# Inverse square roots of spread variances by two ACT functions in place of ACT's square root and DVE's reciprocal, in a three-layer hybrid stack on one core

## The chip, the cores and the metric

One core of a Trainium2 chip runs the whole program in one launch. The metric is the device time of that launch in microseconds (us); lower is better. Engines are named as in the profile: PE (TensorE's matmuls), DVE (VectorE), ACT (ScalarE), POOL (GpSimd), SP (SyncE, which issues the DMAs).

## The reference, cut to what matters

512 tokens of width 1024 pass through two hybrid layers (banded attention, a convolution module and retention side by side, an output projection, then an MLP) and a third layer (differential attention and a state-space branch side by side, then a gated feed-forward). Three places divide by a spread, and the change touches those:

```python
def layer_norm(x):                      # convolution module and retention
    mu = jnp.mean(xf, axis=-1, keepdims=True)
    var = jnp.mean(jnp.square(xf - mu), axis=-1, keepdims=True)
    return (xf - mu) * lax.rsqrt(var + EPS)
...
    y = layer_norm(y) * ln_g + ln_b     # convolution: 256 channels, once a layer
...
    y = layer_norm(y).reshape(b, s, RET_WIDTH)   # retention: 64 channels of each of 6 heads
...
    o = rmsnorm(o, subln_gain[i]) * (1.0 - lam_init)   # differential attention: 128 channels of each of 8 heads
```

## The kernel before, in words

Activations of these branches lie with channels on the partitions and the 512 tokens along the free axis. A mean over channels is therefore a matmul with a matrix of ones: `col_sum` (line 1129) splits the squares into a high part `xhi` and a rest `xlo`, and two matmuls (`xhi,ones` and `xlo,ones`, for retention `xhi,blk64` and `xlo,blk64`) leave the variance in PSUM, already spread over all the partitions that need it. What follows is "variance to inverse root", 128x512 each time, at three places:

- `conv_tail` (lines 1236 and 1237, tile `crs`), once in each of the two hybrid layers;
- `ret_pair` (lines 1322 and 1323, tile `rysq`), for three pairs of heads in each hybrid layer;
- `diff_head` (lines 1848 and 1849, a tile `t`), for the eight heads of the third layer.

That makes 2 + 6 + 8 = 16. In each, ACT takes the square root from PSUM with the constant tile `epsc` as bias, and DVE's `reciprocal` turns it over in place; then DVE multiplies (`ry` by `rysq`, `cacc` by `crs`, `osb` by `t`).

All large matmuls are done as three products of high and low parts: weights arrive by DMA as `wraw`, ACT or DVE makes `whi` (a CAST), DVE or POOL the rest `wlo`; activations are `hhi` and `hlo`. These are the main line of the program. The branches named above run beside it as side tasks. Their own tiles are: `stk` and `khi`, `klo` (a head's queries and keys, copied from PSUM), `row` (scores, then their exponentials), `pthi`, `ptlo` (transposed probabilities), `olow` and `o` (output of a head), `cacc`, `csq` (convolution), `ysq`/`rysq` and `ry` (retention), `do`, `osb` (differential attention).

Nothing is issued in program order. `Trace` records every instruction with the time by which it is wanted, `order` (line 443) plays a list schedule through with its own costs, and `issue` (line 642) issues in the order found. So every instruction has line 642 in the profile, and tiles tell them apart. An engine runs its list strictly in that order: one that waits holds up all behind it. Copies and subtractions of split tiles may go to either of two engines, whichever the planner thinks is done first. PE has 4 PSUM slots for the main line and 4 for side tasks.

ACT's functions come in sets, and a load of a set (ACT_TABLE_LOAD) stands ahead of an activation whose function is not in the set loaded. The program's builder places these loads after the order is fixed; the planner estimates them by a table of its own (lines 670 to 679, used at line 577): where the name of the set changes, it adds 1290 ns.

```python
TABLE = {AF.Exp: "exp", AF.Sigmoid: "sigmoid", AF.Silu: "silu", AF.Sqrt: "sqrt", AF.Sin: "sin",
         AF.Gelu_apprx_tanh: "gelu"}
TABLE_LOAD = 1290.0
...
                        f = table(op) if op.eng[1] == "activation" else None
                        if f and f != loaded:
                            c += TABLE_LOAD
                            loaded = f
```

It costs a DVE reciprocal of n columns at 6.26 n + 65 ns, and an activation at 0.833 n plus some tens of ns.

Of the kernel before, what the change touches and what calls it, by code (L numbers as in the profile page):

```python
# [13 lines left out]
AF = mybir.ActivationFunctionType  # L14
# [3 lines left out]
P = 128  # L18
# [206 lines left out]
class View:  # L225
    """A view of a tile that is traced before the tile is placed."""
# [47 lines left out]
    def mask(self):  # L274
        """First and last column, and which ones between unless it's all."""
        c = self.cols.ravel()
        lo, hi = int(c.min()), int(c.max()) + 1
        if hi - lo == c.size:
            return lo, hi, None
        m = np.zeros(self.t.ncols, bool)  # L280
        m[c] = True
        return lo, hi, None if m[lo:hi].all() else m
# [47 lines left out]
class DramView(View):  # L330
    """A view of a tile in DRAM: taken as a whole."""
# [20 lines left out]
class Pool:  # L352
    """Equal slots, which the order of instructions deals out to tiles. Each is a pool of one buffer."""
# [46 lines left out]
class Trace:  # L400
    """Records instructions with the time by which each is wanted, orders them, and issues them."""
# [207 lines left out]
    def room(self, op, new, live, front, state):  # L609
        """Whether slots are free, none is kept for a more urgent instruction, and enough are left  # L610
        for the instructions before in program order."""
# [58 lines left out]
TABLE = {AF.Exp: "exp", AF.Sigmoid: "sigmoid", AF.Silu: "silu", AF.Sqrt: "sqrt", AF.Sin: "sin",  # L670
# [138 lines left out]
class Builder:  # L809
# [132 lines left out]
    # ---------------------------------------------------------------- norms  # L942
# [116 lines left out]
    # ---------------------------------------------------------------- attention helpers  # L1059
# [41 lines left out]
    def v_pack(self, src):  # L1101
        """V of six heads, each as 64 columns of high parts and 64 of low parts."""
        nc = self.nc
        out = []
# [9 lines left out]
    def pv_pair(self, h, pts, V, y):  # L1114
        """One head's output, from the products with the high and the low parts of V below each other."""
        nc = self.nc
# [7 lines left out]
        a = slice(64 * (h % 2), 64 * (h % 2) + 64)  # L1124
        low = self.s2(name="olow")
# [8 lines left out]

    def rows(self, third):
        """Room for the four rows of blocks of a lower triangle."""
        a, b = self.s2(name="row"), self.s2(name="row")
        return [a[:, 384:512], third, a[:, 0:384], b]

    def p_split(self, parts):  # L1140
        """High and low parts by blocks of keys: 512, 384 and twice 256 columns, the last with a block of zeros."""
        out = []
# [8 lines left out]
        last = out.pop()  # L1151
# [48 lines left out]
    # ---------------------------------------------------------------- conv module  # L1200
# [15 lines left out]
    def conv_tail(self, l):  # L1216
        nc = self.nc
# [18 lines left out]
        nc.scalar.activation(rs, var, AF.Sqrt, bias=self.epsc)  # L1236
        nc.vector.reciprocal(rs, rs)
# [11 lines left out]
    # ---------------------------------------------------------------- retention  # L1249
# [29 lines left out]
    def ret_pair(self, p, q, k):  # L1279
# [42 lines left out]
        nc.scalar.activation(ysq, var, AF.Sqrt, bias=self.epsc)  # L1322
        nc.vector.reciprocal(ysq, ysq)
# [13 lines left out]
    # ---------------------------------------------------------------- hybrid layer  # L1337
    def hybrid(self, l):
# [69 lines left out]
        # output projection and residual  # L1408
# [34 lines left out]
    # ---------------------------------------------------------------- MLP  # L1443
# [80 lines left out]
    # ---------------------------------------------------------------- SSM parameters  # L1524
# [158 lines left out]
    # ---------------------------------------------------------------- SSM  # L1683
# [84 lines left out]
    # ---------------------------------------------------------------- differential attention  # L1768
# [21 lines left out]
    def diff_head(self, h, dqk, V):  # L1790
# [57 lines left out]
        nc.scalar.activation(sq, var, AF.Sqrt, scale=1.0 / P, bias=self.epsc)  # L1848
        nc.vector.reciprocal(sq, sq)
# [230 lines left out]
```

## Time and profile before

| | us |
|---|---|
| runs of the kernel before | 2184.87, 2181.4, 2181.93 |
| their median | 2181.93 |
| span of the profiled execution, first to last instruction | 2185.0 |
| PE busy in it | 2065.8 |
| DVE busy | 1395.2 |
| ACT busy | 928.5 |
| POOL busy | 745.5 |

The profiled execution's own time outside its span isn't given; its span of 2185.0 us stands beside the slowest of the three runs (2184.87 us) and 3.1 us over the median. Busy times are sums over one execution. An engine's share of the whole says little here, because the program goes through stages with different limits: the stages with the 16 places of the change are 130 to 190 us (hybrid layer 0), 780 to 840 us (hybrid layer 1) and 1460 to 1710 us (differential heads).

### The profile page before, as it was taken

Reading aid. Unit: us, or ns where it says so; the run is one execution under the profiler, and the core shown is the slowest. Engines: PE = TensorE matmul, PEld = TensorE weight load, DVE = VectorE, ACT = ScalarE, POOL = GpSimd, SP = SyncE. Lnnn points to the kernel's source line nnn. Section 1 sums busy time; section 2 is a strip of 40 time slices with the busy share of each in tenths; the row PEclk is TensorE's granted clock in tenths of the full one; section 3 lists DMA queues with packets and bytes.
Section 4 is the critical chain, followed back from the end, with each engine's and each line's share of the span. In section 5 each row is a group of like instructions: output and inputs, shape, how many; then the busy total and the mean of one; then the engine's idle time right before and its main releaser. Section 6 shows DMA issues by size and latency. Waiting matters only on the chain. (4 is left out here: it accounts for less than half of the span.)

```text
span 2185.0 us, 27033 instructions
## 1 busy us (share of the span) xinstructions
PE 2065.8 (95%) x9964; PEld 1711.6 (78%) x9964; DVE 1395.2 (64%) x2131; ACT 928.5 (42%) x1521; POOL 745.5 (34%) x858
## 2 busy tenths in 40 slices
PE   7789989899999799989999998999999999999999
PEld 7777878778888777788888877677777788888887
DVE  6999596344457999573444464379888646655545
ACT  3267544232234267454222344456578324433332
POOL 3663357980004663210000115764643431000000
PEclk9999999999999999999999999999999999999999
DMA  5223233332333224133332346222224533333222
GB/s 176 80 78 123 87 116 109 128 127 87 97 114 97 87 68 135 49 107 97 96 97 77 115 133 201 79 80 68 92 82 135 169 96 97 97 96 97 87 87 77
DMA packets 85556, 225.16 MB, mean 103 GB/s; under 512 B 10416, under 2 KB 20400, under 8 KB 85424
## 3 DMA queue, kind: packets, MB, share of 16 engines
q1 hardware_dynamic: 85424, 223.43, 32.4%
q8 instruction: 79, 1.29, 0.3%
q14 instruction: 53, 0.43, 0.1%
HBM read 204.25 MB, written 19.14 MB: 102 GB/s over the span
## 5 line engine op out<-in xcount | busy, mean ns | idle before, releaser
L642 POOL TENSOR_TENSOR wlo<-wraw,whi 128x1024 fp32r<-128x1024 f32 (+1 forms) x156 | 374.5, 2408 | 1068.3 <-ACT whi L642 824.9
L642 ACT CAST whi<-wraw 128x1024 fp32r<-128x1024 f32 (+1 forms) x323 | 330.4, 1029 | 726.7 <-PE ps L642 592.1
L642 PE MATMUL ps<-hhi,whi 128*128 128x512 f32 (+1 forms) x1488 | 506.8, 370 | 7.3 <-DVE acc L642 3.1
L642 PE MATMUL ps<-hlo,whi 128*128 128x512 f32 (+1 forms) x1488 | 504.8, 370 | 5.6 <-DVE hlo L642 5.6
L642 PE MATMUL ps<-hhi,wlo 128*128 128x512 f32 (+1 forms) x1488 | 504.3, 369 | 0.3 <-DVE wlo L642 0.3
L642 PEld LDWEIGHTS ps<-hhi,whi 128*128 128x128 f32 x1488 | 272.4, 191 | 54.8 <-issue 4.0
L642 PEld LDWEIGHTS ps<-hlo,whi 128*128 128x128 f32 x1488 | 272.4, 191 | 53.5 <-DVE hlo L642 6.8
L642 PEld LDWEIGHTS ps<-hhi,wlo 128*128 128x128 f32 x1488 | 272.1, 191 | 48.2 <-DVE wlo L642 1.0
L642 DVE TENSOR_TENSOR wlo<-wraw,whi 128x1024 fp32r<-128x1024 f32 x178 | 223.4, 1257 | 114.8 <-ACT whi L642 114.5
L642 PE MATMUL ps<-whi,fhi 128*128 128x512 f32 x688 | 249.7, 392 | 6.1 <-DVE t L642 3.7
L642 PE MATMUL ps<-whi,flo 128*128 128x512 f32 x688 | 249.5, 391 | 0.0
L642 PE MATMUL ps<-wlo,fhi 128*128 128x512 f32 x688 | 249.5, 391 | 0.0
L642 PE MATMUL ps<-wlo,hhi 128*128 128x384 f32 (+1 forms) x448 | 162.7, 380 | 18.3 <-POOL wlo L642 18.1
L642 DVE TENSOR_TENSOR acc<-ps,acc 128x512 f32<-128x512 f32 x112 | 76.5, 687 | 154.7 <-PE ps L642 154.7
L642 PE MATMUL ps<-whi,hhi 128*128 128x384 f32 (+1 forms) x448 | 161.7, 383 | 14.2 <-DVE rotb L642 12.7
L642 PE MATMUL ps<-whi,hlo 128*128 128x384 f32 (+1 forms) x448 | 158.8, 377 | 0.0
L642 PEld LDWEIGHTS ps<-whi,fhi 128*128 128x128 f32 x688 | 129.6, 189 | 34.7 <-DVE t L642 4.2
L642 PEld LDWEIGHTS ps<-wlo,fhi 128*128 128x128 f32 x688 | 129.6, 189 | 27.8
L642 PEld LDWEIGHTS ps<-whi,flo 128*128 128x128 f32 x688 | 129.5, 188 | 27.8
L642 DVE SCALAR_TENSOR_TENSOR cacc<-cy,pv,cacc 128x509 f32<-128x509 f32 (+26 forms) x120 | 125.3, 1088 | 0.6
L642 POOL TENSOR_TENSOR st<-st,mhalf 128x1 f32<-128x1 f32 (+1 forms) x56 | 54.9, 981 | 194.4 <-DVE st L642 190.8
L642 PEld LDWEIGHTS ps<-wlo,hhi 128*128 128x128 f32 x448 | 86.9, 195 | 30.6 <-POOL wlo L642 21.6
(250 smaller groups left out, 3167.8 us busy)
## 6 DMA issues: line engine op xcount, KB each, us to landing
wraw<-in_wst SPq DMA_DIRECT2D x302, 512.0 KB, 3.5
wraw<-in_wst SPq DMA_DIRECT2D x32, 384.0 KB, 3.1
gain<-in_gains SPq DMA_DIRECT2D x20, 256.0 KB, 4.2
X<-in_x SPq DMA_DIRECT2D x16, 256.0 KB, 6.1
xd<-X SPq DMA_DIRECT2D x16, 256.0 KB, 2.0
X<-xd SPq DMA_DIRECT2D x16, 256.0 KB, 4.9
gated<-t SPq DMA_DIRECT2D x16, 256.0 KB, 2.4
gate<-gated SPq DMA_DIRECT2D x16, 256.0 KB, 3.7
```

Of the source, the lines that this page charges most:

```text
L642: getattr(getattr(self.nc, e), m)(*[r(x) for x in op.args], **{k: r(v) for k, v in op.kw.items()})
```

## The change

A helper takes the natural logarithm of variance plus epsilon from PSUM, and then, in place, the exponential of minus half of it, both on ACT. The planner's table names the logarithm's set "exp", as it does the exponential's, and no longer lists the square root. The rest of the difference is removed doc strings.

```diff
-TABLE = {AF.Exp: "exp", AF.Sigmoid: "sigmoid", AF.Silu: "silu", AF.Sqrt: "sqrt", AF.Sin: "sin",
+TABLE = {AF.Exp: "exp", AF.Sigmoid: "sigmoid", AF.Silu: "silu", AF.Ln: "exp", AF.Sin: "sin",
          AF.Gelu_apprx_tanh: "gelu"}
...
+    def rsqrt(self, out, var, scale=1.0):
+        self.nc.scalar.activation(out, var, AF.Ln, scale=scale, bias=self.epsc)
+        self.nc.scalar.activation(out, out, AF.Exp, scale=-0.5)
...
-        nc.scalar.activation(rs, var, AF.Sqrt, bias=self.epsc)
-        nc.vector.reciprocal(rs, rs)
+        self.rsqrt(rs, var)
...
-        nc.scalar.activation(ysq, var, AF.Sqrt, bias=self.epsc)
-        nc.vector.reciprocal(ysq, ysq)
+        self.rsqrt(ysq, var)
...
-        nc.scalar.activation(sq, var, AF.Sqrt, scale=1.0 / P, bias=self.epsc)
-        nc.vector.reciprocal(sq, sq)
+        self.rsqrt(sq, var, 1.0 / P)
```

Since costs and sets are other for the planner, the order of all engines changes from the first of the 16 places on. In the built program the loads of function sets are 41 before and 68 in the change. The planner's choices move 10 of the 323 `whi` casts and 5 of the 8 `hhi<-osb` casts from ACT to DVE, and 4 of 178 `wlo` subtractions from DVE to POOL.

ACT in hybrid layer 0, from the last retention pair's work to the convolution's two SiLUs (`cacc`). The forms with `epsc` are the square roots before, and the logarithms in the change. Before:

```order
L642 ACTIVATE rysq<-ps,epsc 128x512
L642 COPY olow<-o 64x512 x2
L642 ACTIVATE stk<-ps 64x512 x2
L642 CAST whi<-wraw 128x1024
L642 ACTIVATE rysq<-ry 128x512
L642 CAST khi<-ps 64x512
L642 CAST xhi<-rysq 128x512
L642 CAST khi<-ps 64x512 x3
L642 CAST whi<-wraw 128x1024
L642 ACTIVATE rysq<-ps,epsc 128x512
L642 ACT_TABLE_LOAD
L642 ACTIVATE cacc<-cacc,pv 128x512 x2
```

Here the square roots of a pair stand apart, attention's `stk` and `khi` copies between them, with one load, for the SiLU. The change, from the same `xhi<-rysq` to the same SiLUs:

```order
L642 CAST xhi<-rysq 128x512
L642 ACT_TABLE_LOAD
L642 ACTIVATE crs<-ps,epsc 128x512
L642 ACT_TABLE_LOAD
L642 ACTIVATE crs<-crs 128x512
L642 ACT_TABLE_LOAD
L642 ACTIVATE rysq<-ps,epsc 128x512
L642 CAST whi<-wraw 128x1024
L642 ACT_TABLE_LOAD
L642 ACTIVATE rysq<-rysq 128x512
L642 ACT_TABLE_LOAD
L642 ACTIVATE cacc<-cacc,pv 128x512 x2
```

Five loads stand there now, one ahead of every logarithm, every exponential and the SiLUs; the `stk` and `khi` copies of the next attention head have moved behind them. Hybrid layer 1 has the same twelve rows in the same order.

DVE at the same place, from the convolution's inverse root to the first `klo` of the attention head. Before:

```order
L642 RECIPROCAL crs<-crs 128x512
L642 TENSOR_TENSOR ry<-o,olow 64x512 x2
L642 RECIPROCAL rysq<-rysq 128x512
L642 TENSOR_TENSOR xlo<-rysq,xhi 128x512
L642 TENSOR_TENSOR ry<-ry,rysq 128x512
L642 TENSOR_TENSOR cacc<-cacc,crs 128x512 x2
L642 RECIPROCAL rysq<-rysq 128x512
L642 TENSOR_TENSOR mixlo<-cacc,mixhi 128x512
L642 TENSOR_TENSOR ry<-ry,rysq 128x512
L642 TENSOR_TENSOR mixlo<-cacc,mixhi 128x512
L642 SCALAR_TENSOR_TENSOR stk<-ps,stk 64x512 x2
L642 TENSOR_TENSOR klo<-ps,khi 64x512 x4
```

The change:

```order
L642 TENSOR_TENSOR ry<-o,olow 64x512 x2
L642 TENSOR_TENSOR xlo<-csq,xhi 128x512
L642 TENSOR_TENSOR xlo<-rysq,xhi 128x512
L642 TENSOR_TENSOR cacc<-cacc,crs 128x512 x2
L642 TENSOR_TENSOR ry<-ry,rysq 128x512
L642 CAST whi<-wraw 128x1024
L642 TENSOR_TENSOR mixlo<-cacc,mixhi 128x512 x2
L642 SCALAR_TENSOR_TENSOR stk<-ps,stk 64x512 x2
L642 TENSOR_TENSOR klo<-ps,khi 64x512 x4
```

The reciprocals are gone from the list, and DVE takes over a `whi` cast that ACT had.

ACT in the third layer, behind the exponentials of the second differential head. Before:

```order
L642 ACTIVATE row,st<-row,st,rq 128x512
L642 ACT_TABLE_LOAD
L642 ACTIVATE t<-ps,epsc 128x512
L642 ACT_TABLE_LOAD
L642 ACTIVATE t<-ps 128x512
L642 CAST pthi<-ps 128x512
L642 CAST pthi<-ps 128x384 x2
L642 CAST stk<-ps 64x512 x2
L642 CAST whi<-wraw 128x1024
```

The change (`t<-ps,epsc` is the first head's logarithm, `t<-t` its exponential, `t<-ps` the sigmoid of a gate):

```order
L642 ACTIVATE row,st<-row,st,rq 128x512
L642 ACT_TABLE_LOAD
L642 ACTIVATE t<-ps,epsc 128x512
L642 CAST whi<-wraw 128x1024
L642 ACT_TABLE_LOAD
L642 ACTIVATE t<-t 128x512
L642 ACT_TABLE_LOAD
L642 ACTIVATE t<-ps 128x512
L642 CAST stk<-ps 64x512
L642 CAST pthi<-ps 128x512
L642 CAST pthi<-ps 128x384 x2
```

Two loads have become three, with the exponential between them.

## Rows read from the trace of the kernel before

**Rows 1.** The profile page's head: the span, busy time of each engine (share of the span, count of instructions), and the span in 40 slices of 54.6 us, each digit the busy share of a slice in tenths (9 is 90% or more).

```profile
span 2185.0 us, 27033 instructions
PE 2065.8 (95%) x9964; PEld 1711.6 (78%) x9964; DVE 1395.2 (64%) x2131; ACT 928.5 (42%) x1521; POOL 745.5 (34%) x858
PE   7789989899999799989999998999999999999999
DVE  6999596344457999573444464379888646655545
ACT  3267544232234267454222344456578324433332
```

**Rows 2.** Busy time by stretch: from:to, length, then busy us (count of instructions) of PE, PEld, DVE, ACT, POOL, then the granted clock, DMA share and GB/s.

```profile
130.00:190.00 60.00, 57.79 (x282) 47.91 (x281) 57.04 (x83) 46.83 (x81) 36.79 (x66) 0.97 0.27 84
190.00:250.00 60.00, 56.30 (x293) 45.76 (x292) 48.59 (x116) 41.03 (x89) 14.59 (x6) 1.00 0.28 93
780.00:840.00 60.00, 58.63 (x296) 48.39 (x295) 56.68 (x77) 50.31 (x85) 34.99 (x67) 1.00 0.33 103
840.00:900.00 60.00, 52.63 (x263) 42.16 (x261) 52.95 (x120) 42.01 (x91) 19.00 (x8) 0.98 0.26 82
1460.00:1710.00 250.00, 235.89 (x1128) 189.77 (x1128) 212.34 (x398) 171.08 (x320) 118.77 (x84) 1.00 0.31 98
150.00:160.00 10.00, 7.90 (x32) 6.19 (x31) 9.90 (x8) 6.72 (x12) 6.14 (x9) 0.83 0.37 124
210.00:220.00 10.00, 7.26 (x38) 5.23 (x37) 9.78 (x23) 8.20 (x20) 2.40 (x1) 1.00 0.22 73
550.00:600.00 50.00, 50.00 (x220) 40.84 (x219) 21.74 (x25) 13.18 (x16) 2.70 (x1) 1.00 0.31 94
```

**Rows 3.** What PE waited for in 1460 to 1710 us: us in total, times, longest.

```profile
PE ps L642 <- DVE row L642: 7.4, 6, 2.1
PE ps L642 <- DVE klo L642: 2.2, 3, 1.0
...
PE ps L642 <- DVE t L642: 1.4, 1, 1.4
```

**Rows 4.** The same for 840 to 900 us.

```profile
PE ps L642 <- DVE row L642: 3.2, 4, 1.8
PE ps L642 <- DVE klo L642: 2.9, 2, 1.5
```

**Rows 5.** DVE in order of time in hybrid layer 0: start us, us (of all in a merged row), engine, line, op, out<-in, count, idle before and releaser.

```profile
155.03 3.34 DVE L642 RECIPROCAL rysq<-rysq 128x512 f32<-128x512 f32 x1
158.29 1.81 DVE L642 TENSOR_TENSOR ptlo<-ps,pthi 128x512 fp32r<-128x512 f32 x3
161.13 1.79 DVE L642 TENSOR_TENSOR ptlo<-ps,pthi 128x512 fp32r<-128x512 f32 x3 [1.02 <-ACT pthi L642]
```

**Rows 6.** DVE's groups by tile over the whole span: form, count | busy us, mean ns of one | idle before, releaser.

```profile
L642 DVE RECIPROCAL t<-t 128x512 f32<-128x512 f32 x8 | 26.8, 3350 | 3.5 <-ACT t L642 3.5
L642 DVE RECIPROCAL rysq<-rysq 128x512 f32<-128x512 f32 x6 | 20.1, 3350 | 2.4 <-ACT rysq L642 2.3
L642 DVE RECIPROCAL crs<-crs 128x512 f32<-128x512 f32 x2 | 6.7, 3336 | 0.0
L642 DVE CAST whi<-wraw 128x1024 fp32r<-128x1024 f32 x11 | 7.7, 704 | 5.8 <-POOL wlo L642 2.5 <-PE ps L642 1.9 <-issue 1.3
```

**Rows 7.** ACT's groups by tile and form over the whole span, same columns.

```profile
L642 ACT CAST whi<-wraw 128x1024 fp32r<-128x1024 f32 x291 | 304.0, 1051 | 647.1 <-PE ps L642 535.5 <-DVE X L642 61.1 <-issue 37.6
L642 ACT ACT_TABLE_LOAD x41 | 52.6, 1283 | 8.7 <-DVE st L642 7.2 <-PEq L2072 0.8
L642 ACT ACTIVATE t<-t 128x512 f32<-128x512 f32 x64 | 40.5, 633 | 2.0
...
L642 ACT ACTIVATE row<-row,st,rq 128x512 f32<-128x512 f32 x16 | 12.9, 808 | 0.0
...
L642 ACT ACTIVATE t<-ps,epsc 128x512 f32<-128x512 f32 x8 | 5.5, 689 | 1.6 <-PE ps L642 1.5
...
L642 ACT CAST hhi<-osb 128x512 fp32r<-128x512 f32 x8 | 4.7, 627 | 1.4 <-DVE osb L642 0.8 <-PE ps L642 0.6
...
L642 ACT ACTIVATE rysq<-ps,epsc 128x512 f32<-128x512 f32 x6 | 4.1, 688 | 7.5 <-PE ps L642 7.4
```

**Rows 8.** ACT in order of time in hybrid layer 0, columns as in Rows 5.

```profile
148.22 1.99 ACT L642 CAST whi<-wraw 128x1024 fp32r<-128x1024 f32 x2
150.23 1.28 ACT L642 ACT_TABLE_LOAD   x1
151.52 0.69 ACT L642 ACTIVATE rysq<-ps,epsc 128x512 f32<-128x512 f32 x1
...
167.74 1.19 ACT L642 COPY olow<-o 64x512 f32<-64x512 f32 x2 [1.97 <-PE o L642]
...
177.67 1.52 ACT L642 ACTIVATE cacc<-cacc,pv 128x512 f32<-128x512 f32 x2
179.10 1.13 ACT L642 CAST mixhi<-cacc 128x512 fp32r<-128x512 f32 x2
...
181.08 1.19 ACT L642 ACTIVATE stk<-ps 64x512 fp32r<-64x512 f32 x2
...
183.42 1.78 ACT L642 CAST khi<-ps 64x512 fp32r<-64x512 f32 x3
```

## The prediction on record

> **What bounds the kernel now.** I read the page's head first [rows 1]: PE is busy 95% of the span, so a change on ACT and DVE can win only where PE stands still, and lose only by making it stand still more. A slice is 54.6 us: PE reads 7 or 8 in slices 1 to 3, 6, 8, 14, 18 and 25 and 9 elsewhere, too coarse for our places, but DVE reads 8 or 9 just there (slices 2 to 4, 14 to 16 and 28 to 31: 55 to 218, 710 to 874, 1475 to 1693 us) and in slice 6, while ACT reads 8 once and 7 or less elsewhere.
>
> So next I cut the span at the stages of the 16 inverse roots [rows 2]. Length less PE's busy time is PE's idle time: 2.2 us in 130 to 190, 1.4 us in 780 to 840, 14.1 us in 1460 to 1710, together 17.7 us. Behind the first two, where attention's side tasks run out, PE idles another 3.7 us (190 to 250) and 7.4 us (840 to 900). These 28.8 us are all that the change can win directly. DVE is the fullest of the helpers there: 95% and 94% of the first and third of these stretches, 85% of the heads' 250 us, against 78%, 84% and 68% for ACT.
>
> Who ends PE's waits says the same. In the heads' stretch it is DVE's `row`, `klo` and `t`, 11.0 of the 14.1 us [rows 3]; behind hybrid layer 1 `row` and `klo`, 6.1 of 7.4 [rows 4]. No wait of weight there is put down to ACT. A DVE reciprocal is long (3.34 us) and the list is strict: in layer 0 three `ptlo` subtractions start at 158.29, when the reciprocal in front of them ends, and the next three stand behind those [rows 5].
>
> **What DVE loses.** 16 reciprocals, 26.8 + 20.1 + 6.7 = 53.6 us [rows 6]: 13.4 us in each hybrid layer, 26.8 us in the heads. The planner gives DVE ten more `whi` casts at 704 ns, 7.0 us [rows 6], and five `hhi` casts.
>
> **What ACT gains.** A logarithm in place of a square root: the trace has no logarithm. Its nearest row is the square root itself, same shape, PSUM source and `epsc` bias, 688 to 689 ns [rows 7]; so nothing is added, and I bound the difference by 0.1 us either way. The exponential in place: nearest is the 128x512 square from SBUF, 633 ns; the long end is the `row` exponential with two pointers, 808 ns [rows 7]. I take 0.63: 16 x 0.63 = 10.1 us. Loads: 68 - 41 = 27 more at 1.283 us = 34.6 us [rows 7]. Together 44.7 us; the casts that move away take 10 x 1.05 + 5 x 0.63 = 13.6 us off again [rows 7]. Net ACT +31, DVE -44 (and a few `wlo` that go to POOL): the two come nearer to each other, and the question is what PE sees.
>
> **How dear a load is.** In rows, a load follows the cast in front of it within 0.02 us and the activation starts 1.29 us after the load did [rows 8]; no other gap is there. The Trainium skill (ScalarE: Activation LUTs, section What ACT_TABLE_LOAD costs) has the same 1283 ns, but adds a drain of about 1380 ns to each switch; by that page, an estimate, 27 loads would cost ACT 72 us, which speaks against the change, and the rows do not bear it out. The sum goes by the rows' 1.29.
>
> **What the planner does not see.** Its table now puts logarithm and exponential in one set. The built order has a load ahead of nearly every one of either. Going through the 68 loads by the planner's table leaves 43, so 25 are not in its plan: 7 in each hybrid layer and 11 in the heads. PE's list is laid out for a plan in which ACT is earlier.
>
> **Hybrid layers, by hand.** From the end of the third pair's `xhi` the new ACT list runs: 5 loads 6.45, 2 logarithms 1.38, 2 exponentials 1.26, one `whi` 1.05, two SiLUs 1.52, two `mixhi` 1.13, two `stk` 1.19, two of the four `khi` 1.19 [rows 7, 8]; 15.2 us, less about 0.6 for the overlap that two casts show (1.99 us for two of 1.05). So attention's first scores can start after some 14.6 us. PE's new list has 42 matmuls from that `xhi` to these scores; at the full stages' 220 in 50 us [rows 2] PE is there in 9.5 us. It waits about 5.1 us. Before that, the logarithm and exponential of the second pair, a load and two `olow` stand ahead of the convolution's `xhi`: 0.69 + 1.29 + 0.63 + 1.19 + 0.64, with handovers some 4.6 us, against 20 smaller matmuls, 3.9 us: a wait of 0.7. Each layer: 5.8 us of idle in place of 2.2 and 1.4, so **+3.6 and +4.4 us**.
>
> What comes back: in PE's list the last value product of attention now stands 3.7 us (layer 0) and 8.6 us (layer 1) of matmuls earlier than before, since the plan has a freer DVE. The idle stretches behind, 3.7 and 7.4 us [rows 2], are mostly waits for DVE at the tail of these tasks. I take back half: **-1.9 and -3.7 us**; bounds are none and all of it.
>
> **Heads.** 11 unplanned loads are 14.2 us. ACT is only 68% full here, its gaps absorb some, and sigmoids of gates have slack, so I let half reach PE: **+7.1**. Of PE's 14.1 us of idle, waits for DVE behind chains that reciprocals shared; I take half: **-7.1**. Bounds are 0 to 14 for each.
>
> The moved casts have their cover: `whi` is made ahead in four buffers, and 0.70 us on DVE takes the place of 1.05 on ACT; should that cover go, ten times 0.7 us is at stake. Work outside these stretches keeps its durations.
>
> **Sum.** 3.6 + 4.4 - 1.9 - 3.7 + 7.1 - 7.1 = +2.4 us. PE's idle also moves its clock: in 150 to 160 us it idled 2.1 us and the mean grant was 0.83, between the 1.2 and 2.4 GHz levels, in 210 to 220 it idled 2.7 us and the grant was 1.00 [rows 2]. At 0.83 ten microseconds lose 1.7 us of work. Waits of 5 us in one piece are longer than today's there, so I add one such loss: **+4.1 us**. From the profiled span, 2185.0, that gives 2189.1; that execution stands 3.1 us over the median of the runs, so on the median 2181.9 + 4.1 = **2186.0 us**. 0.2% is 4.4 us, about what a measurement of this kernel tells from no change.
>
> **Rivals.**
> *All loads reach PE (0.24).* ACT becomes the bound in the hybrid clusters and each unplanned load in front of `khi` or the exponentials is a wait. Mechanism and price: 3.6 + 4.4 + 3.4 for the clock, nothing back at the tails, 14.2 in the heads: +25.6, 2207 at worst; with half of the DVE relief in the heads, +18.5, 2200. For it: ACT's 14.6 us against PE's 9.5. Against: ACT at 171 of 250 us in the heads. It decides where the loads of a head stand ahead of its exponentials with no gap behind them. This is the other side of the next one.
>
> *DVE's relief wins (0.20).* Waits for DVE go: two thirds of 14.1 + 3.7 + 7.4 is -16.8, and the clusters cost only 2 us a layer because DVE, no longer in 3.35 us pieces [rows 6], catches up: -13, 2169. For it: DVE's 94 to 95% and the releasers [rows 3, 4]. Against: PE idles only 2.2 and 1.4 us in the very stretches of the hybrid layers' reciprocals.
>
> *The loads cost nothing (0.03).* Were the 25 unplanned loads not to run, or to be no-ops because the set is there already, each cluster would shrink by 5 x 1.29 = 6.5 us, so its wait and the clock's 1.7 us vanish, and with them the heads' +7.1: -3.6 - 3.7 - 1.9 - 7.1 + 0.7 = about -16, 2166. Against: the built order has the loads, and every one of the 41 in the trace takes its 1283 ns [rows 7]. The Trainium skill (ScalarE: Activation LUTs, section Table sets: the hidden batching unit) says that one set holds both functions, so that the pair needs one load; this rule would give that time, and the built order contradicts it.
>
> *A load holds ACT twice as long (0.03).* If something behind each load took as long again, 1.28 us, five in each cluster would add 6.4 us to PE's wait in each layer and half of 17 more loads in the heads 10.9: 4.1 + 12.8 + 10.9 = +27.8, 2210. Against: the activation that starts 1.29 us after its load [rows 8]. The skill's drain, from above, is this case.
>
> **Numbers.** My forecast (0.50) is a trade with a small loss: within 0.2% for 0.36, slower by more for 0.13, faster by more for 0.01. Slower: 0.13 + 0.24 + 0.03 = 0.40. Faster: 0.01 + 0.18 (the relief; its weak end, 0.02, stays within) + 0.03 = 0.22. Within: 0.36 + 0.02 = 0.38. The range goes from most of the relief case to the milder slower case: 2172 to 2200. The forecast's own range is 2179 to 2193.
>
> **What would show it.** ACT_TABLE_LOAD x68 at 1283 ns with no gap behind; no 128x512 RECIPROCAL; ACT near 960 us, DVE near 1350. In 130 to 200 and 780 to 850 us PE should wait some 5 us at attention's first scores, released by ACT's `khi` or DVE's `klo` behind it. The tails behind should idle less than 3.7 and 7.4 us. In the heads, PE's waits for `row` and `klo` should be about as long as before. I am wrong if PE's idle in the hybrid stretches stays under 2.5 us a layer (ACT's lag is absorbed), if that of the heads falls below 7 us or grows past 20, or if the time moves by idle of PE in stages that have none of the 16.

## The result: slower by 1.15%, and the profile after

The changed kernel takes **2208.99 us** (median, 2207.67 to 2210.25) where the kernel before takes 2183.4 beside it (2181.4 to 2189.26): ratio 1.0115, 95% interval 1.0099 to 1.013. The forecast was 2186.0 us in a range of 2172 to 2200. It was wrong. All medians here are of fast executions; two slow ones, of 2539 us (old heads, below) and 10196 us (the kernel before), are left out.

The head of the page after, with the slices that answer to [rows 1]:

```profile
span 2208.3 us, 27033 instructions
PE 2078.8 (94%) x9964; PEld 1727.7 (78%) x9964; DVE 1368.8 (62%) x2124; ACT 961.1 (44%) x1551; POOL 755.4 (34%) x862
PE   7788989999999788999999998989999999999999
DVE  6987586444447987463444564468778646655555
ACT  3277534222234277544322344447579424433322
```

The span is 23.3 us longer. TensorE's 9964 matmuls are the same, yet its busy time rises by 13.0 us (2078.8 - 2065.8) and its idle time by only 10.3 us (129.5 - 119.2). More than half of the loss is the same matmuls taking longer, not waiting; the mean granted clock over the span is 0.974 where it was 0.983.

The stretches that answer to [rows 2] (length, busy us and count of PE, PEld, DVE, ACT, POOL, then the granted clock, DMA share, GB/s), and the loads of ACT's tables, which answer to [rows 7]:

```profile
130.00:190.00 60.00, 53.53 (x253) 44.02 (x252) 41.14 (x77) 50.63 (x79) 31.60 (x58) 0.94 0.21 62
190.00:250.00 60.00, 54.17 (x274) 44.71 (x273) 51.57 (x112) 41.30 (x95) 14.22 (x7) 0.94 0.30 100
780.00:840.00 60.00, 54.91 (x273) 46.36 (x271) 42.28 (x69) 51.34 (x82) 36.95 (x76) 0.94 0.20 62
840.00:900.00 60.00, 52.40 (x253) 42.45 (x253) 54.15 (x122) 41.29 (x92) 13.71 (x7) 0.94 0.32 106
...
550.00:600.00 50.00, 50.00 (x220) 40.85 (x218) 24.24 (x27) 15.29 (x18) 2.70 (x1) 1.00 0.29 89
```

```profile
L642 ACT ACT_TABLE_LOAD x68 | 87.2, 1283 | 4.8 <-DVE st L642 2.1 <-PEq L2074 0.8 <-PE ps L642 0.8
```

DVE is relieved (57.04 to 41.14 us in the first stretch), ACT is fuller, and TensorE idles 6.5, 5.8, 5.1 and 7.6 us where it idled 2.2, 3.7, 1.4 and 7.4. The clock falls to 0.94 in all four. In a stretch with none of the roots, 550 to 600, TensorE does as before: 220 matmuls, no idle time, full clock.

ACT in hybrid layer 0, in order of time, columns as in [rows 5], beside [rows 8]:

```profile
157.60 1.28 ACT L642 ACT_TABLE_LOAD   x1 [0.77 <-PE ps L642]
158.90 0.69 ACT L642 ACTIVATE rysq<-ps,epsc 128x512 f32<-128x512 f32 x1
159.60 1.28 ACT L642 ACT_TABLE_LOAD   x1
160.90 0.63 ACT L642 ACTIVATE rysq<-rysq 128x512 f32<-128x512 f32 x1
161.56 1.19 ACT L642 COPY olow<-o 64x512 f32<-64x512 f32 x2
162.77 0.62 ACT L642 CAST xhi<-csq 128x512 fp32r<-128x512 f32 x1
...
165.44 1.28 ACT L642 ACT_TABLE_LOAD   x1
166.73 0.69 ACT L642 ACTIVATE crs<-ps,epsc 128x512 f32<-128x512 f32 x1
167.44 1.28 ACT L642 ACT_TABLE_LOAD   x1
168.74 0.63 ACT L642 ACTIVATE crs<-crs 128x512 f32<-128x512 f32 x1
169.38 1.28 ACT L642 ACT_TABLE_LOAD   x1
170.68 0.69 ACT L642 ACTIVATE rysq<-ps,epsc 128x512 f32<-128x512 f32 x1
...
172.32 1.28 ACT L642 ACT_TABLE_LOAD   x1
173.62 0.63 ACT L642 ACTIVATE rysq<-rysq 128x512 f32<-128x512 f32 x1
174.27 1.28 ACT L642 ACT_TABLE_LOAD   x1
```

Every logarithm and every exponential shown has a load of its own. A load takes 1.28 us, the activation starts 1.29 to 1.30 us after the load did, the next load directly behind it. TensorE feels this; what it waits for in 130 to 190 us (us in total, times, longest):

```profile
PE ps L642 <- ACT khi L642: 3.5, 1, 3.5
PE ps L642 <- ACT xhi L642: 2.2, 1, 2.2
```

`xhi` is the cast at 162.77 behind two loads, `khi` the one behind the five from 165.44 on. In hybrid layer 1 the same two waits are 1.9 and 3.2 us, but the one at `khi` falls behind the cut at 840 us. TensorE's waits in 840 to 900 us, then the two stretches cut at 850, before and after:

```profile
PE ps L642 <- DVE row L642: 4.7, 2, 2.6
PE ps L642 <- ACT khi L642: 3.2, 1, 3.2
```

```profile
780.00:850.00 70.00, 68.63 (x347) 56.70 (x346) 63.85 (x96) 57.19 (x99) 41.75 (x69) 1.00 0.34 106
850.00:900.00 50.00, 42.63 (x212) 33.85 (x210) 45.79 (x101) 35.13 (x77) 12.24 (x5) 0.97 0.23 74
```

```profile
780.00:850.00 70.00, 62.81 (x304) 53.01 (x303) 50.76 (x87) 56.67 (x90) 38.09 (x77) 0.93 0.20 61
850.00:900.00 50.00, 44.50 (x223) 35.81 (x221) 45.67 (x104) 35.96 (x84) 12.57 (x6) 0.97 0.35 116
```

With the wait at `khi` counted to the cluster of roots that it follows, TensorE idles 7.2 us there after (1.4 before) and 5.5 us behind it (7.4 before).

Last the heads, from the first transpose of `dqk` on TensorE to the last product with `mhi`; before, then after:

```profile
1428.60:1811.90 383.30, 366.68 (x1721) 295.26 (x1719) 287.16 (x492) 214.02 (x382) 177.50 (x126) 1.00 0.32 103
```

```profile
1442.20:1835.70 393.50, 373.84 (x1720) 301.21 (x1719) 275.71 (x491) 234.41 (x398) 185.53 (x131) 0.98 0.31 102
```

So the 23.3 us lie in two places: 13.6 before the heads begin (1428.6 to 1442.2) and 10.2 in the heads, of which 7.2 are longer matmuls and 3.0 idle. What follows gains half a microsecond.

### The profile page after: what moved, and what is told of

It is laid out like the page before. It is cut to its first block, busy times and chain, and to the rows that moved or that the text cites. A ratio compares the mean times of both kernels' runs of the same rounds, so it can differ in the third digit from the quotient of the medians.

```text
span 2208.3 us, 27033 instructions
## 1 busy us (share of the span) xinstructions
PE 2078.8 (94%) x9964; PEld 1727.7 (78%) x9964; DVE 1368.8 (62%) x2124; ACT 961.1 (44%) x1551; POOL 755.4 (34%) x862
## 3 DMA queue, kind: packets, MB, share of 16 engines
q8 instruction: 79, 1.29, 0.2%
## 5 line engine op out<-in xcount | busy, mean ns | idle before, releaser
L642 POOL TENSOR_TENSOR wlo<-wraw,whi 128x1024 fp32r<-128x1024 f32 (+1 forms) x160 | 384.1, 2407 | 1087.3 <-ACT whi L642 810.6
L642 ACT CAST whi<-wraw 128x1024 fp32r<-128x1024 f32 (+1 forms) x313 | 320.1, 1029 | 745.2 <-PE ps L642 621.7
L642 DVE TENSOR_TENSOR wlo<-wraw,whi 128x1024 fp32r<-128x1024 f32 x174 | 219.4, 1262 | 119.5 <-ACT whi L642 119.2
L642 PE MATMUL ps<-whi,hhi 128*128 128x384 f32 (+1 forms) x448 | 156.5, 387 | 5.7 <-DVE rotb L642 5.4
```

The lines of the kernel that those rows point to most:

```text
L642: getattr(getattr(self.nc, e), m)(*[r(x) for x in op.args], **{k: r(v) for k, v in op.kw.items()})
```

## Experiments

"Begin" is the shift of the heads' first transpose against before's 1428.6 us, so the cost of all that comes earlier; "heads" is the length of the stage just shown (383.3 us before). The kernel before took 2184.1 to 2184.5 us beside these runs. Begin, heads and busy time are read from one profiled execution of each kernel.

| kernel | median us | ratio, 95% | loads | begin | heads | PE busy / idle against before |
|---|---|---|---|---|---|---|
| after | 2209.0 | 1.0099-1.0130 | 68 | +13.6 | 393.5 | +13.0 / +10.3 |
| one set, new order | 2194.2 | 1.0032-1.0062 | 42 | -1.8 | 393.3 | +4.8 / +2.8 |
| planner told of two sets | 2201.1 | 1.0063-1.0093 | 64 | +6.2 | 392.0 | +12.3 / +2.1 |
| before, loads only | 2198.7 | 1.0047-1.0081 | 64 | +3.5 | 392.0 | +4.5 / +7.2 |
| before, relief only | 2181.4 | 0.9979-0.9997 | 41 | -8.1 | 384.9 | -4.0 / -3.0 |
| pair, old lists, one set | 2189.4 | 1.0014-1.0033 | 45 | +0.2 | 384.3 | +1.1 / -0.4 |
| pair, old lists, two sets | 2199.4 | 1.0050-1.0083 | 64 | +9.6 | 388.2 | +6.6 / +7.9 |
| re-planned, price -1% | 2188.3 | 1.0009-1.0028 | 39 | -6.1 | 390.2 | +4.0 / -3.1 |
| re-planned, price +0.9% | 2187.8 | 1.0004-1.0023 | 39 | -8.3 | 393.9 | -0.5 / +2.3 |
| one set, waits filled | 2199.7 | 1.0054-1.0081 | 42 | +5.4 | 392.2 | +13.5 / +0.9 |
| one set, old heads | 2187.6 | 1.0006-1.0026 | 39 | -3.8 | 387.5 | +3.6 / -3.3 |
| layers re-planned | 2180.8 | 0.9974-0.9992 | 39 | -6.2 | 383.3 | +0.4 / -7.1 |
| one set, 8 transposes late | 2197.2 | 1.0051-1.0081 | 42 | +2.6 | 391.4 | +8.5 / +2.5 |
| before, 8 transposes late | 2185.8 | 0.9996-1.0015 | 41 | -3.8 | 386.0 | +4.8 / -5.0 |

**One set, new order.** In `issue`, ahead of each run of exponentials or logarithms, a set that holds both is loaded by its name, so that neither loads its own:

```diff
+            f = table(op) if m == "activation" else None
+            if f == "exp" and cur != "exp":
+                self.nc.scalar.preload_act_table_set("natural_log_exp_and_others")
+            cur = f or cur
```

> The changed kernel with every engine's list as it is, but the set that holds both logarithm and exponential is loaded by name wherever either is wanted: 42 loads in place of 68, as the planner assumed. Theory A (loads that the planner did not see make ACT late, PE waits, and each wait brings a stretch at the low TensorE clock): the 25 us of loss vanish and part of DVE's relief shows, 2165 to 2185 us, mean granted clock back to 0.98 or more, PE idle in 130 to 190 us under 3 us. Theory B (the new order is bad by itself, whatever the loads): 2200 to 2210 us, clock 0.975. Theory C (half and half): about 2195 us.

2194.2 us, theory C's time. Of the five loads of a cluster one is left, for the SiLUs, and `khi`'s wait is gone: no `khi` stands among TensorE's waits, and the heads begin 15.4 us earlier than after. Not all of the clusters' idle time goes with them: TensorE still idles 3.8 us in 130 to 190 (theory A said under 3) and 4.8 us in 780 to 850, where it idled 2.2 and 1.4 before. The heads themselves don't change by more than 0.2 us, though twelve of their loads are gone too. So the loads explain when the heads begin, and the heads' 10 us are something else.

**Planner told.** The logarithm gets a table of its own in the planner, as the build has it.

```diff
-... AF.Ln: "exp", ...
+... AF.Ln: "ln", ...
```

> The change with one word other: the planner's table gives the logarithm a set of its own, so the plan knows the loads that the built program has (64 of them by the built order). Theory A1 (what hurts is that the plan is blind to the loads): 2180 to 2192 us, clock about 0.98. Theory A2 (what hurts is ACT's time for the loads, seen or not): 2200 to 2212 us. Theory B (another order is as good or bad as any): anywhere between 2180 and 2215.

2201.1 us, in theory A2's range: with nearly as many loads (64), 7.9 us of the loss go, 7.4 of them before the heads; the heads stay at 392. That the planner places work behind loads it knows of is the likely reason, but no run tells it from the other order that it makes.

**Loads only.** The kernel before, its lists unchanged, with the exponential's set loaded right behind each of the 16 square roots.

```diff
+            if m == "activation" and op.args[2] is AF.Sqrt:
+                ...
+                self.nc.scalar.preload_act_table_set("exp_and_others")
```

> The kernel before with all lists as they are, square roots and reciprocals included, but the exponential's set is loaded right behind each square root: 64 loads in place of 41, 23 more, none in the plan. Theory A: loads alone, without any relief of DVE, cost as much as the change did or more, 2200 to 2220 us, with a mean granted clock of 0.975 or less. Theory B: loads are absorbed in ACT's gaps, 2183 to 2190 us.

2198.7 us, 1.3 under theory A's range and far over theory B's; the mean granted clock is 0.982, not 0.975 or less. 23 loads alone cost 14.2 us, 0.62 us each, half of their 1.283. TensorE idles 7.2 us more and is busy 4.5 us more; 8.7 us of the loss are in the heads.

**Relief only.** The kernel before, its lists unchanged; the 16 reciprocals invert one column, the other 511 stay as they are.

```diff
+            if m == "reciprocal" and op.args[0].n == 512:
+                op.args = [x[:, :1] for x in op.args]
```

> The kernel before with all lists as they are, but the 16 reciprocals of 512 columns work on one column each (the inversion of the other 511 is left out): DVE loses 53 us, nothing else changes. Theory D (DVE's reciprocals hold PE up): 2165 to 2178 us, with fewer waits for row and klo in the heads. Theory A (PE's waits in these stretches are set by chains in which the reciprocal is a small part, and the list was planned around it): 2178 to 2184 us, no gain or up to 5 us.

2181.4 us, in theory A's range. DVE loses 49 us of work (1395.2 to 1346.0) and the kernel gains 3.0. The stretches behind the clusters and the heads, columns as above:

```profile
190.00:250.00 60.00, 56.31 (x293) 45.72 (x292) 47.31 (x113) 41.56 (x89) 14.71 (x7) 1.00 0.27 93
...
840.00:900.00 60.00, 52.56 (x270) 42.52 (x270) 50.96 (x111) 39.97 (x85) 14.62 (x6) 0.97 0.22 71
```

TensorE idles 3.7 and 7.4 us there, to the tenth what it idled before [rows 2]. The waits for DVE's `row` and `klo` there are no waits for a reciprocal: in 840 to 910 us both kernels have 3.2 and 2.9 us of them.

**Pair in the old lists.** The planner still records a square root and a reciprocal and makes before's lists; when they are issued, the logarithm and an exponential on ACT take their places. Once with the set by name, once with the loads that each brings.

```diff
+            if m == "activation" and op.args[2] is AF.Sqrt:
+                op.args = (*op.args[:2], AF.Ln)
+            elif m == "reciprocal" and op.args[0].n == 512:
+                e, m, op.args, op.kw = "scalar", "activation", (*op.args, AF.Exp), {"scale": -0.5}
```

> The planner still records a square root and a reciprocal and makes the lists of the kernel before; only when the instructions are issued does the logarithm take the square root's place and an exponential on ACT, at the reciprocal's place in the order, the reciprocal's. The set with both functions is loaded by name: 45 loads, 4 more than before. So the arithmetic is the changed kernel's, without its new order and without its separate loads. Theory R (of the changed kernel's +25 us some 15 are the separate loads and the other 10 come from the new order that the planner makes when its costs change): 2181 to 2187 us. Theory A (the 10 us come from the exponentials themselves, that ACT does in its own time in place of DVE, and would be there in any order): 2192 to 2197 us, as with one set in the changed kernel's order (2194.2).

> As the run before it, but each function loads the set that the compiler picks for it: 64 loads, as many within four as in the changed kernel (68), in the old order. Theory R: the loads alone, 2195 to 2201 us (23 loads beside the square roots of the kernel before gave 2198.7), less some 3 for the relief of DVE: 2193 to 2199. Theory A: 2205 to 2212, the changed kernel's time. Theory P (the loads are dear only in an order that was planned without them, and the order of before has room for them): 2184 to 2190.

2189.4 and 2199.4 us. The first lies between the two theories, nearer to R, the second just over R's upper end. The pair in one set costs 5 us even in the old order: four loads more than before and 16 exponentials on ACT outweigh the relief of DVE. How the cost divides between loads and exponentials was not tried. The 19 separate loads cost another 10.0. The heads with one set, columns as above:

```profile
1428.80:1813.10 384.30, 366.93 (x1720) 295.08 (x1719) 258.75 (x484) 220.18 (x392) 177.64 (x126) 1.00 0.32 103
```

The pair in the old order leaves the heads at 384 and at full clock; in the new order, with the same arithmetic and one set, they take:

```profile
1426.80:1820.10 393.30, 373.80 (x1720) 301.64 (x1719) 272.55 (x491) 218.67 (x386) 185.94 (x131) 0.98 0.30 102
```

6.9 us more busy time for the same 1720 recorded matmuls, 2.1 us more idle. The heads' loss comes with the new order, and it is mostly longer matmuls.

**Re-planned.** The kernel before, nothing computed otherwise; the planner's price of a 512-column reciprocal, 3270 ns, is moved by some 30 ns down and up.

```diff
-            return 6.26 * n + 65
+            return 6.2 * n + 65      # and 6.3
```

> The kernel before with the planner's price of a reciprocal lowered by 1% (3239 ns in place of 3270 for 512 columns; the trace has 3.34 us). Nothing is computed otherwise and no instruction is dearer; only the order changes, in some 1900 rows of TensorE's list. Theory R in its strong form (any new order of this planner costs some 10 us against the order that stands): 2190 to 2197. Theory A, and R in its weak form (it was this one new order that is bad): 2181 to 2187.

> The same with the price raised by 0.9% (3298 ns): another order, some 1560 rows of TensorE's list changed. Theory R, strong form: 2190 to 2197. Theory A and R in its weak form: 2181 to 2187. With the run before it this tells how far two orders lie apart that differ by nothing but a price of 30 ns.

2188.3 and 2187.8 us, 3.5 to 4 over before and about 1 over the upper end of theory A and the weak form of R; by stage it is more: the heads begin 6.1 and 8.3 us earlier and then take 6.9 and 10.6 us longer. Each of the three new orders of the heads, the changed kernel's and these two, is slower than before's.

**Waits filled.** One set, new order, with 48 transposes of the identity at five places of the heads, into PSUM that the product behind then overwrites.

```diff
+                for _ in range(FILL.get((k, n), 0)):
+                    self.nc.tensor.transpose(r(op.args[0])[:, :P], ident, ident)
+FILL = {("kb", 8): 16, ("row", 120): 8, ("row", 150): 8, ("row", 190): 8, ("do", 12): 8}
```

> One set, the changed kernel's order (2194.2 us before), plus 48 transposes of the identity at five places in the heads' stage where TensorE waits 2.2 to 3.5 us for VectorE and the granted clock is 0.50 for some 3.4 us right after it: 16 ahead of the third block of SSM products (wait of 3.5 us), 8 each ahead of the first transposes of heads 0, 3 and 7 (2.6, 2.2 and 2.4 us) and ahead of head 1's first product with V (2.3 us). They write into the product's own PSUM tile, which is then overwritten, and need nothing that is late, so they run inside the wait; 8 take about 1.0 us. Theory C (the heads' 10 us are not idle time but five to six stretches of the lower clock, 1.7 us each, that the longer waits of the new order bring): the five stretches go, some 8.5 us, 2185 to 2189. Theory W (what is lost is the waits and the order of the work; the clock is a by-product): 2193 to 2199, unchanged or more by the work that was added.

2199.7 us: theory C's time failed, and theory W's range is missed by 0.7 us. Theory C's mechanism shows at two of the five places. Head 0 in the kernel without the fill, in slices of 2 us:

```profile
1472.00:1474.00 2.00, 0.31 (x2) 0.00 (x0) 2.00 (x3) 0.60 (x1) 1.41 (x1) 1.00 0.74 293
1474.00:1476.00 2.00, 1.11 (x7) 0.92 (x8) 2.00 (x6) 0.03 (x1) 0.00 (x0) 1.00 0.53 203
1476.00:1478.00 2.00, 2.00 (x9) 1.59 (x8) 1.97 (x4) 1.59 (x3) 0.91 (x1) 0.57 0.15 59
1478.00:1480.00 2.00, 2.00 (x6) 1.57 (x6) 1.94 (x4) 0.39 (x2) 1.47 (x1) 0.57 0.00 0
```

TensorE stands still for 2.58 us and then works 4 us at 0.57, most of it at the 1.2 GHz level. With the fill, first TensorE's rows, then the slices:

```profile
1479.07 1.03 PE L651 MATMUL ps<-cm 128*128 128x128 f32 x8
1481.72 0.33 PE L654 MATMUL ps<-cm,row 128*128 128x128 f32 x1 [1.62 <-DVE row L654]
```

```profile
1480.00:1482.00 2.00, 0.38 (x3) 0.25 (x2) 2.00 (x7) 0.00 (x0) 0.33 (x1) 1.00 0.64 168
1482.00:1484.00 2.00, 2.00 (x14) 1.57 (x13) 1.99 (x5) 1.13 (x2) 0.01 (x1) 1.00 0.51 203
1484.00:1486.00 2.00, 2.00 (x10) 1.50 (x8) 1.96 (x4) 1.01 (x3) 2.00 (x1) 1.00 0.00 0
```

The eight transposes take 1.03 us of the wait, 1.62 us remain, and the clock stays at 1.00; so it did at heads 3 and 7. At the other two places the fill missed its wait: 16 stood ahead of the SSM block before the one that waits (1.9 us of work for nothing), and those at head 1 started only after the wait; there the clock fell as before. It also fell behind head 5's wait of 2.07 us, behind which it had not fallen in the kernel without the fill: the length of a wait does not settle it alone. The kernel without the fill was built a second time, with eight transposes near its end (below) and the same lists through the heads. There, too, the clock fell at heads 0 and 3; but behind head 7's wait, and behind the longest wait of the stage, 3.5 us ahead of the SSM block, it stayed up without any fill. Head 7 in the first build, then the SSM block and head 7 in the second:

```profile
1699.00:1701.00 2.00, 2.00 (x9) 1.70 (x8) 1.97 (x4) 0.32 (x1) 1.23 (x1) 0.50 1.01 396
```

```profile
1435.00:1437.00 2.00, 2.00 (x7) 1.18 (x8) 2.00 (x4) 1.85 (x3) 1.60 (x2) 1.00 0.10 32
1701.00:1703.00 2.00, 2.00 (x15) 1.75 (x14) 1.97 (x5) 1.10 (x3) 0.57 (x1) 1.00 0.92 360
```

So only heads 0 and 3 speak for the fill. The heads became only 1.1 us shorter with it, and they began 7.2 us later: 1.9 of it is the misplaced fill, but already at the end of layer 1's MLP, ahead of any fill, the kernel was 4.5 us behind the one with the same lists. That was unexpected and called for the last two runs. (The added transposes are in this kernel's busy time.)

**Old heads; layers re-planned.** In the first the pair (one set) is planned as such in the layers only, in the heads as a square root and a reciprocal that are replaced when issued. In the second, the kernel before, the price is raised to 3290 ns for the layers' reciprocals alone. In both, TensorE's list from the heads' first transpose on is before's, row for row.

```diff
-            return 6.26 * n + 65
+            return (6.26 if args[0].t.name not in ('crs', 'rysq') else 6.3) * n + 65
```

> The logarithm and the exponential everywhere, one set by name, but the planner is told of them in the layers only; in the heads it still plans a square root and a reciprocal, so that TensorE's list from the first transpose of the heads on is row for row that of before, and the pair takes their places when they are issued. Theory H (with one set, all of what is left of the slowdown, 10 us, is the heads' new order): the heads take 384 us again in place of 393, 2182 to 2187. Theory S (what is left is spread over the whole kernel and the landmarks' offset is chance): 2189 to 2195.

> The kernel before, square root and reciprocal kept; the planner's price for the reciprocals of the two hybrid layers alone raised by 0.9% (3290 in place of 3270 ns). With the raised price everywhere the heads began 8.3 us earlier than before and took 10 us longer; here TensorE's list in the heads is that of before. Theory H: the layers keep their gain of some 6 us and the heads lose nothing: 2176 to 2181, under both kernels. Theory S: as with the price raised everywhere, 2185 to 2191.

2187.6 us, a little over theory H's 2182 to 2187: the heads take 387.5 in place of 393.3, not 384. And 2180.8 us, within theory H's range: the layers keep their 6.2 us, the heads take 383.3. This is the version under both kernels, by 28 us against the changed one and by 0.17% (0.08 to 0.26) against before; it keeps square root and reciprocal. The medians show the heads' order without any stage length: one set and one set with old heads have the same TensorE list up to 1390 us and end 6.5 us apart; price +0.9% and layers re-planned have the same list up to 1397 us and end 6.9 us apart.

**The spread between builds.** Eight transposes, 1 us at most, in the closing MLP of one set (new order) and of before.

```diff
+                for _ in range(LATE.pop(0) if k == "fhi" and n >= 1200 and op.kw.get("start") and LATE else 0):
+                    self.nc.tensor.transpose(r(op.args[0])[:, :P], ident, ident)
```

> The kernel with one set and the changed kernel's order (2194.2 us), with 8 transposes of the identity added in one place, ahead of a product of the closing MLP; every list is the same up to there, some 400 us before the end, and the 8 cost 1 us at most (8 took 1.03 us where they stood alone). With the filled waits the time was 2199.7 though its lists were the same up to the heads, and its heads began 7.2 us later. Theory B (two builds with the same lists differ by some microseconds, by how the granted clock falls in the stages that nothing changed): any time from 2190 to 2201 but not 2193 to 2197, and heads that begin over 3 us off 1426.8. Theory F (the filled waits themselves made the layers slower, through something that runs ahead of them): 2193 to 2197, heads within 2 us of 1426.8.

> The same 8 transposes at the like place of the kernel before, all else as before. Theory B: up to 5 us off the kernel before on either side, heads that begin over 2 us off 1428.6. Theory F: 2183 to 2187, heads within 2 us of 1428.6. With the run beside it this says how far a difference between two single kernels may be read.

2197.2 and 2185.8 us, with heads that begin 4.4 us later and 3.8 us earlier than in the kernel that has the same lists up to there. By the landmarks theory B holds, and the fill need not be blamed for what came ahead of it; by the times the first lies just over the edge between the theories and the second within theory F, 3.0 and 1.5 us over their twins, 1 us of it the added work. The eight stand some 124 us before the end, not 400, so the heads have the same lists too; those of the second build with one set take 391.4 us, not 393.3.

Where two such builds drift apart, the granted clock has fallen in one and not in the other. One set, first and second build:

```profile
465.00:485.00 20.00, 17.63 (x76) 14.32 (x77) 10.99 (x12) 6.73 (x9) 16.72 (x37) 1.00 0.33 110
```

```profile
465.00:485.00 20.00, 17.44 (x69) 13.70 (x68) 9.33 (x9) 5.28 (x6) 19.09 (x42) 0.91 0.24 81
```

Between 439 and 512 us the second falls 2.1 us further behind. What decides where the clock falls is open, and with one profile each, a difference between builds is not told from one between executions. A stage that differs by some 4 us between two single profiles is therefore no effect by itself; what is read from a stage below shows in several kernels at once. The gains of 3.0 us (relief only) and 3.5 us (layers re-planned) are little more than two builds of the same lists differ by.

## Why the prediction was wrong, step by step

**Where the loss comes from.** Between kernels that differ in nothing else, the separate loads cost 10.0 us (old lists) or 12 to 15 us (new order, against the two builds with one set and no filled waits); the pair in place of square root and reciprocal, in one set and the old order, 5 us; the new order with one set another 5 to 7. Together that is the 25, each part with an uncertainty of some 2 us, by which builds with the same lists differ.

**The step that failed.** The forecast took back 12.7 us of waiting for the relief of DVE (1.9 + 3.7 at the tails, 7.1 in the heads), and it left the planner's new order of the heads and the lower clock behind longer waits out of the sum, but for 1.7 us. The whole relief, taken alone, moved the time by 3.0 us; the new order costs 5 to 9 us in the heads, and TensorE's busy time rose by 13.0 us.

The sum, with what took each term's place, from the two profiled executions (span +23.3):

| term | forecast us | measured us |
|---|---|---|
| clusters in the layers (idle, 130-190 and 780-850) | +3.6, +4.4 | +4.3, +5.8 |
| tails (idle, 190-250 and 850-900) | -1.9, -3.7 | +2.1, -1.9 |
| heads, loads and relief | +7.1 - 7.1 | +3.0 idle, +7.2 busy |
| longer matmuls (clock) elsewhere | +1.7 | +5.8 |
| idle elsewhere | 0 | -3.0 |

- **The clusters were right in kind and near in size.** 6.5 and 7.2 us of idle where the working said 5.8 and 5.8. Its parts were a longer wait at `xhi` (2.2 and 1.9, not 0.7) and a shorter one at `khi` (3.5 and 3.2, not 5.1). About half of the rise is the new order's: with one set 3.8 and 4.8 us are left. A load's price of 1.29 us was right too, so the rival of a load that holds ACT twice as long is out.
- **"I take back half" of the tails failed.** Behind layer 0 nothing came back; behind layer 1 half of what was taken did, but not by the relief: the relief alone leaves both tails at 3.7 and 7.4 us (190 to 250 and 840 to 900), while in the new order the waits for `klo` there are gone and those for `row` are longer. The step read a wait for DVE as a wait for what DVE was relieved of.
- **"I take half" of the heads' waits failed.** With the relief alone the heads idle 16.0 us (384.9 - 368.90) after 16.6. The releasers of [rows 3] named the engine rightly and the reason wrongly: whatever makes DVE late there, it is not the reciprocals. What does was not followed.
- **The heads' loads, +7.1, are not settled.** With before's order, ten more loads in the heads cost 3.9 us in one pair of builds (388.2 - 384.3) and 8.7 in the other (392.0 - 383.3, loads only); in the new order twelve more cost 0.2 to 2.1 (393.5 against 393.3 and 391.4). Heads of the same list and without separate loads lie up to 4 us apart.
- **The order was taken as neutral.** It is other from 92 us on for TensorE, 60 us ahead of the first root at 151.5, and not only from the first of the 16 places on, as the section on the change has it. The forecast counted what moves in the layers by hand, and in the heads only durations. The planner's new heads cost some 5 to 9 us by themselves: 391.4 to 393.3 with the pair and one set, 390.2 and 393.9 without any change of arithmetic, where before's order takes 383.3 to 387.5, 384.9 on average, in six builds without separate loads. Why the planner's new lists put TensorE in front of `row` and `kb` for longer was not followed further.
- **The clock's term, +1.7 for one low stretch, was mis-sized most.** TensorE's busy time rose by 13.0 us. In the heads the new order idles only 3.0 us more but in longer pieces, and the granted clock falls behind them: 0.98 in place of 1.00 over the stage, 7.2 us of the 10.2. The row that the step rested on, 2.7 us of idle at a grant of 1.00 [rows 2], was two waits of 1.2 us and one of 0.3; a single wait of 2.58 us here is followed by some 4 us at 0.57. But such a wait does not always bring the fall. Before's own heads have waits of 2.5 and 2.1 us; the clock falls behind both in four of the eight builds with its list and behind neither in the other four, before among them. The second of them, in before and in before with eight transposes late:

```profile
1471.00:1473.00 2.00, 1.76 (x12) 1.37 (x12) 2.00 (x5) 0.00 (x0) 0.00 (x0) 1.00 0.64 256
```

```profile
1471.00:1473.00 2.00, 2.00 (x9) 1.52 (x8) 1.96 (x4) 1.10 (x2) 0.00 (x0) 0.62 0.00 0
```

So the order alone does not fix the clock's 7.2 us: in the second build with one set and the new order, the heads' busy time is 3.0 us less (370.8, not 373.8).
- **Of the signs, ACT's held and DVE's did not.** ACT is at 961.1 us (960 was said), DVE at 1368.8 (1350). The ten `whi` casts added 10.7 us where 7.0 was reckoned, the five `hhi` casts 6.3, and 28 small scalings of `st`, the same instructions as before, take 18.2 us where they took 7.2; why is open.

Of the rivals, that all loads reach TensorE gave 2200 to 2207, nearly the measured size by another road: it put 7 to 14 us of loads on the heads, where order and clock were what came. That the relief wins is out at 2181.4 us with all relief and no load. That the loads cost nothing was tried directly: with one set the waits at `khi` go, as it said, but the time is 2194, not 2166, since the relief it counted on isn't there and the new order stays. The rule on one set in the Trainium skill (ScalarE: Activation LUTs, section Table sets: the hidden batching unit) holds for the pair only where that one set is what is loaded: 42 loads with the set named, 68 without.

## What to carry to other kernels

A wait that is put down to an engine says who was late, not that less work of another kind on that engine would end it: before counting a relief, look for the removed instruction in the chain ahead of the late one, or take its work out alone and see. Where the engine that bounds the kernel has a clock that can fall behind its waits, price a longer wait twice, for itself and for the slower work that may follow it, and compare busy time as well as idle time. A change of costs in a planner is a change of order everywhere, so try the new order without the change (a price moved by 1%) and the change in the old order.

## What the runs showed of the hardware that was not expected

- Longer matmuls cost as much as the waits. Between before and after, +10.3 us of idle came with +13.0 us of longer matmuls; 23 loads in before's lists brought +7.2 and +4.5.
- More work can keep the clock: 1.03 us of transposes inside a wait of 2.6 us left 1.62 us of idle and the grant at 1.00, where 4 us at 0.57 had followed; so at two heads whose wait brought the fall in both builds without the fill. In the time of this one build it did not show.
- Kernels with the same lists up to the heads reach them up to 4.4 us apart (-1.8 and +2.6 us with one set, 0 and -3.8 with before's lists, one profile each), though no engine's list differs ahead of that point; the stretches at a lower clock do.
- 49 us less of DVE's work, in stretches where it was up to 95% busy [rows 2], were worth 3.0 us.
- The fall of the clock behind one and the same wait is not fixed: behind waits of 2.5 and 2.1 us it came in four of eight builds with the same TensorE list, and a wait of 3.5 us was once followed by none.
